# A decoder layer on one core: accumulating transfers from a negated cast, rotations moved into the products that need them, two copies on another engine

## The chip, the cores and the metric

The kernel runs on one core of a Trainium2 chip. A core has a matrix engine (PE, with its weight loads PEld), a vector engine (DVE), a scalar engine (ACT), a general engine (POOL) and an engine that here only issues transfers (SP). Each works through its own list of instructions in order and waits on semaphores for the others. Data moves between the chip's memory (HBM) and the core's on-chip memory (SBUF) by 16 DMA engines, whose transfers are issued from the queues of SP, ACT or POOL. Products of PE land in eight banks of PSUM, which DVE and ACT read.

The metric is the device time of one execution in microseconds; a measurement is the median of several.

## The reference

One layer for 256 positions and a width of 2048, all in float32:

```python
h = layer_norm(alpha * h + 0.5 * swiglu(h, w_ffn1_gu[i], w_ffn1_down[i]), ln_g[i, 0], ln_b[i, 0])
rq, rk, rv, rg, aq, ak, av, gate_r, gate_a = jnp.split(h @ w_in[i], SPLIT_POINTS, axis=-1)
rq = rotary(rq.reshape(B, S, RET_HEADS, RET_DK), positions, RET_DK, RET_THETA)
rk = rotary(rk.reshape(B, S, RET_HEADS, RET_DK), positions, RET_DK, RET_THETA) * (RET_DK ** -0.5)
...
ro = head_group_norm(retention_chunkwise(rq, rk, rv), ret_gn_g[i]).astype(h.dtype)
ret_branch = (jax.nn.silu(rg) * ro) @ w_ret_out[i]
...
att_branch = sliding_window_attention_sinks(aq, ak, av, att_sinks[i]) @ w_att_out[i]
mixed = (jax.nn.sigmoid(gate_r) * ret_branch + jax.nn.sigmoid(gate_a) * att_branch) @ w_mix_out[i]
h = layer_norm(alpha * h + mixed, ln_g[i, 1], ln_b[i, 1])
h = layer_norm(alpha * h + 0.5 * swiglu(h, w_ffn2_gu[i], w_ffn2_down[i]), ln_g[i, 2], ln_b[i, 2])
ple = jax.nn.sigmoid(h @ w_ple_gate[i]) * (p[i] @ w_ple_proj[i])
h = layer_norm(alpha * h + ple, ln_g[i, 3], ln_b[i, 3])
```

The FFNs have an inner width of 5632. Retention has 8 heads (128 for queries and keys, 256 for values), the attention 16 query heads and 4 key heads of 64. The rotary embedding turns pairs of a vector's elements by an angle that grows with the position, so it needs a table of cosines and sines for the 256 positions.

## The kernel before

**Split operands.** A float32 product is made of three products of a faster format: every operand is split into a high part (a rounded copy, made by ACT) and a low part (what is left, made by DVE as a subtraction), in `split` at line 100. `Sum.add` (line 417) then runs three matrix products: low times high (L426), high times high (L427), and, last, high times the weight's low part (L428). For features computed with the roles exchanged (`features_chunk`, names rqk and aqk) a chunk runs eight products with the weight's high part (L377) and then the low ones (L385).

**Weights.** All weights stream from HBM in chunks of 128 partitions x 1024 elements, 512 KB. A plan lists them in the order of use. `fill` looks at it after each chunk that PE has finished (`done`): it loads the next chunks on SP's queue into one of 46 slots, and makes (splits) the chunks whose turn is near, so that some four chunks stand made ahead of PE. Names say what a tile is: rf_gu is the raw chunk of an FFN's gate and up weights, hf_gu its high part, lf_gu its low part; rw_in_f and so on for the mixers' input weights.

**Kinds of units.** In the FFNs' gate and up products, column blocks of 512 are worked off unit by unit. Some units are plain. Some ("S", class `Seven`) save one of eight products by adding weight halves first (tiles uf_gu and vf_gu, lines 222 to 225). In some pairs ("F") the second chunk, the "up" one, is `Folded`: its low part is not subtracted by DVE. ACT writes the high part (L165) and then its negative into the low part's tile (L166), and POOL issues a transfer that adds the raw chunk to it on its way (L167), so that raw minus high is left. There are 43 such chunks. Column blocks end with sums of the partial results on DVE (evw, eve, line 1026).

**The order around the products.** The engines' lists follow the program text, so the text is the schedule. `run_side` is called after every chunk of the long products: it runs the next job of `side` (retention and attention steps) and one step of the first generator in `lazy`. In `lazy` stand `rotary_table` (the angles; name "r" for retention, "a" for attention; ten steps of small DVE instructions, two sines on ACT and a load of the positions on ACT's queue) and `sums_ahead` (line 271), which makes the sums of the "D" units of the second FFN early and stores them to HBM: per item two loads, four adds, two high parts on ACT, two subtractions (L300, L302) and four stores, in steps that are two or three chunks apart.

**The stages of `mixers`** are: the first value block (rv); eight groups of query and key features (rqk, four chunks each, groups 0 to 3 the queries, 4 to 7 the keys); three more value blocks of eight chunks; the retention gate (rg) with the heads' scores (rs) and outputs (ro) between its chunks; attention features (av, aqk); the four blocks of retention's outer gate (gt) with eight steps of the attention between them; two gate blocks of the attention side (ga0, ga1); then the output products. The retention table "r" is made in the first FFN's down projection, from its first unit on. After each rqk group, `rotated` joins its two PSUM halves (ACT copies one, DVE adds, `joined`) and rotates at once: a shuffle, two multiplications and an addition on DVE (lines 1127 to 1131). An attention step runs the scores (as), a softmax on DVE and ACT (asc, aes), a transposition by DMA (wat to mat), a copy back on ACT (apt, L197) and the output product (ao). The gate blocks gt are copied out of PSUM by ACT (sig, L1460). Ahead of the third and the fourth of them DVE makes sums of activations for `Seven` units (`forms_of`, gaf0 and gaf1, from L511 on).

Of the kernel before, what the change touches and what calls it, by code (L numbers as in the profile page):

```python
# [8 lines left out]
F32 = mybir.dt.float32  # L9
# [4 lines left out]
ALU = mybir.AluOpType  # L14
# [44 lines left out]
def layer(ctx: ExitStack, tc: tile.TileContext, io):  # L59
    nc = tc.nc  # L60
    sync, act, dve, pool, pe = nc.sync, nc.scalar, nc.vector, nc.gpsimd, nc.tensor
# [14 lines left out]
    def slot(shape, dt, name):  # L76
        return slots.tile(shape, dt, tag="slot", name=name)

    def half(name):
        return slot([P, 2, 256], F32, name)  # L80
# [23 lines left out]
    class Chunk:  # L104
# [18 lines left out]
        def make(self):  # L123
            self.make_hi()
            split(self.hi, self.lo, self.raw)
# [24 lines left out]
    class Folded:  # L150
# [11 lines left out]
        def make(self):  # L162
            c = self.chunk
            c.make_hi()
            act.copy(c.hi, c.raw)  # L165
            act.mul(c.lo, c.hi.bitcast(F32), -1.0)  # L166
            pool.dma_start(c.lo, c.raw, accum_op=ALU.add)  # L167

    class Turn:

# [100 lines left out]
    def sums_ahead(items, wait, every):  # L271


        def pause():
            for _ in range(every):
                yield

        pairs = [[Chunk(k) for k in items[0]]]
        for _ in range(wait):
            yield  # L280
        for j, (key, _) in enumerate(items):
            a, b = pairs.pop()
            b11, b21, b12, b22 = a.of(a.raw, 0), a.of(a.raw, 1), b.of(b.raw, 0), b.of(b.raw, 1)
            u, v = (slot([P, 2, 512], F32, w + a.name) for w in "uv")
            t1, t3, t2, t4 = (x.rearrange("p (g n) -> p g n", g=2) for x in (u[:, 0], u[:, 1], v[:, 0], v[:, 1]))
            parts = [slot([P, 2, 512], F32R, w + a.name) for w in ("hu", "lu", "hv", "lv")]
            uh, ul, vh, vl = parts
            away = [dram.tile([P, 2, 512], F32, name=f"{w}{a.name}") for w in ("hud", "lud", "hvd", "lvd")]
            put_by_sums[key] = away
            dve.tensor_tensor(t1, b11, b12, ALU.add)  # L290
            dve.tensor_tensor(t3, b12, b22, ALU.add)
            yield from pause()
            act.copy(uh, u)
            dve.tensor_tensor(t2, b11, t3, ALU.add)
            dve.tensor_tensor(t4, t2, b21, ALU.add)
            yield from pause()
            act.copy(vh, v)
            if j + 1 < len(items):
                pairs.append([Chunk(k) for k in items[j + 1]])
            dve.tensor_tensor(ul, u, uh, ALU.subtract)  # L300
            yield from pause()
            dve.tensor_tensor(vl, v, vh, ALU.subtract)  # L302
            for e in range(2):
                sync.dma_start(away[e], parts[e].bitcast(F32))
            yield from pause()
            for e in range(2, 4):
                sync.dma_start(away[e], parts[e].bitcast(F32))
# [48 lines left out]
        room["quiet"] = on  # L356

    side = []
    lazy = []
    idle = lambda: None  # L360

    def run_side(n=1):
        for _ in range(n):
            if side:
                side.pop(0)()
        if lazy and next(lazy[0], "end") == "end":
            lazy.pop(0)

    def features_chunk(key, n_k, rhs, ps):
        c, chunks = key[-1], n_k // 4  # L370
# [480 lines left out]
    trig = {}  # L851
# [16 lines left out]
    def rotary_table(nm):  # L868

        inv, sgn = (0, 2) if nm == "r" else (1, 3)  # L870
        pos_i = slot([P, S], I32, "pos_i" + nm)
        act.dma_start(pos_i, io["positions"].broadcast_to([P, S]))
        pos = slot([P, S], F32, "pos" + nm)
        yield
        dve.tensor_copy(pos, pos_i)
        table = slot([P, 2, S], F32, "trig" + nm)
        cos, sin = trig[nm] = table[:, 0, :], table[:, 1, :]
        w = slot([P, 4, S], F32, "rot" + nm)
        ang, n, na, nb = (w[:, j, :] for j in range(4))
        dve.tensor_scalar(ang, pos, cst[:, inv : inv + 1], None, ALU.mult)  # L880
        dve.tensor_scalar(n, ang, INV_2PI, MAGIC, ALU.mult, ALU.add)
        dve.tensor_scalar(n, n, MAGIC, None, ALU.subtract)
        dve.tensor_scalar(na, n, 1.0 / 2048.0, MAGIC, ALU.mult, ALU.add)
        dve.tensor_scalar(na, na, MAGIC, 2048.0, ALU.subtract, ALU.mult)
        dve.tensor_tensor(nb, n, na, ALU.subtract)
        yield
        for who, j in ((na, 0), (nb, 0), (na, 1), (nb, 1), (na, 2), (nb, 2), (na, 3)):
            dve.scalar_tensor_tensor(ang, who, -TWO_PI[j], ang, ALU.mult, ALU.add)
            if who is nb:
                yield  # L890
        yield
        dve.tensor_scalar(n, ang, 3.1415925, -3.1415925, ALU.min, ALU.max)
        yield
        act.activation(nb, n, AF.Sin)
        yield
        dve.tensor_scalar(sin, nb, cst[:, sgn : sgn + 1], None, ALU.mult)
        dve.tensor_scalar(na, ang, 1.5707963267948966, None, ALU.add)
        dve.tensor_scalar(n, na, 3.141592653589793, -6.283185307179586, ALU.is_gt, ALU.mult)
        dve.tensor_tensor(na, na, n, ALU.add)
        dve.tensor_scalar(na, na, 3.1415925, -3.1415925, ALU.min, ALU.max)  # L900
        yield
        act.activation(cos, na, AF.Sin)
        yield
# [47 lines left out]
    def ffn(name, i, ht, norm, keep, residual, keepers, away):  # L951
# [105 lines left out]
            return f  # L1057

        def before_unit(u):
            if u == 0 and name == "f1":  # L1060
                lazy.append(rotary_table("r"))
            g = u // 2 + 2
            others(2 * KF // 4 - max(0, KF // 4 - 1 - g) + (2 if u >= 10 else 0))
            if u % 2 == 0:
                if 2 <= u < 2 + 2 * len(SEVEN_DOWN):
                    at = u // 2 - 1
                    made[SEVEN_DOWN[at]] = seven_forms(raws[SEVEN_DOWN[at]], space[:, 2 * at], space[:, 2 * at + 1])
                if g < KF // 4:
                    convert(g)
            if u in (11, 12):  # L1070
                y[u - 11] = load_columns(residual, u - 11, name + "y")
# [44 lines left out]
    def joined(ps, name, dst=None):  # L1116
        lo = half(name + "lo")
        v = half(name + "v") if dst is None else dst
        for f in range(2):
            act.copy(lo[:, f], ps[f][:, S:])  # L1120
            dve.tensor_tensor(v[:, f], ps[f][:, :S], lo[:, f], ALU.add)
        return v

    def rotate(ps, name, dst, cos, sin, shuffle):
        q = joined(ps, name)
        qs = half(name + "sh")
        dve.stream_shuffle(qs, q, shuffle)
        c, s = (v[:, None, :].broadcast_to([P, 2, S]) for v in (cos, sin))
        dve.tensor_tensor(q, q, c, ALU.mult)
        dve.tensor_tensor(qs, qs, s, ALU.mult)  # L1130
        dve.tensor_tensor(dst, q, qs, ALU.add)

    SH_R = [(i + 16) % 32 for i in range(32)]
    SH_A = [i + 8 if i < 8 else i - 8 if i < 16 else i for i in range(32)]
# [35 lines left out]
        side.insert(n, job)  # L1170

    def mixers(ht, norm, residual, keepers, away):
        cos_r, sin_r = trig["r"]
        rhs = lambda k: (ht[:, k, :S], ht[:, k, S:])
        both_halves = lambda k: ht[:, k, :]
        rq = [slot([P, 4, S], F32, f"rq{j}") for j in range(2)]
# [1 line left out]

        def rotated(grp, ps):
            who = (rq, rk)[grp // 4][grp % 4 // 2]  # L1180
            rotate(ps, f"rr{grp}", who[:, grp % 2 * 2 : grp % 2 * 2 + 2, :], cos_r, sin_r, SH_R)

        rv = []

# [6 lines left out]
        ps = banks("rv0")  # L1191
# [5 lines left out]
        for c in range(FRONT, KD // 2):  # L1197
            u = take(("w_rv", 0, c))
# [2 lines left out]
        values(0, ps)  # L1201
        slots_for_weights(14)
        ahead = [(gu_keys("f2", j)(0, p), gu_keys("f2", j)(1, p)) for j in AHEAD for p in AHEAD[j]]
        lazy.append(sums_ahead(ahead[:2], 3, 2))
        lazy.append(rotary_table("a"))
        lazy.append(sums_ahead(ahead[2:5], 2, 2))
        lazy.append(sums_ahead(ahead[5:8], 2, 3))
        for grp in range(8):
            ps = banks(f"rqk{grp}")
            features_out([(("w_in_f", grp), ps)], KD, both_halves)  # L1210
            rotated(grp, ps)
        grp = 8
# [3 lines left out]
        for blk in range(1, 4):  # L1216
            ps = banks(f"rv{blk}")
# [97 lines left out]
        for h in range(0, HR, 2):  # L1315
            ps = banks(f"rg{h}")
# [6 lines left out]
            c = h // 2  # L1323
# [5 lines left out]
        ps = banks("av")  # L1329
# [119 lines left out]
        sig = []  # L1449
        for j in range(4):  # L1450
            def before(c, j=j):
                if c == 0 and j >= 2:
                    g = j - 2
                    made[g] = forms_of([ht[:, 4 * g : 4 * g + 4, :]], f"gaf{g}")

            ps = banks(f"gt{j}")
            paired_out(("w_in_f2", 21 + 2 * j), KD, rhs, ps, before)
            sig.append(slot([P, 2, 512], F32, f"sig{j}"))
            for t in range(2):
                act.copy(sig[-1][:, t], ps[t])  # L1460
        assert not side

        def mixer_block(name, units, keys, lhs):
# [38 lines left out]
        for b in range(2):  # L1502
# [3 lines left out]
            for n in range(2):  # L1506
                j = 2 * b + n
# [31 lines left out]
        ps = banks("mo2")  # L1539
# [4 lines left out]
        ps = banks("mo3")  # L1544
# [4 lines left out]
        for c in range(first):  # L1549
            u = take(("w_mix", 3, c))  # L1550
# [311 lines left out]
```

## Time and profile before

| | |
|---|---|
| median of three runs | 2252.4 us (2251.03 to 2253.74) |
| the profiled execution | 2251.64 us |
| its span | 2249.9 us, so 1.7 us lie outside the span |
| granted PE clock | 0.999 |
| HBM read, written | 484.43 MB, 29.36 MB |
| mean transfer rate | 248 GB/s |

The page divides the span into 40 slices. In its row for PE every slice but the last shows nine tenths or more; DVE's digits lie between seven and nine in most slices, ACT's between four and seven. A matrix product on 512 columns shows as 0.39 us, but such products overlap in the pipeline and start 0.22 to 0.23 us apart. In rows of stretches, the number behind an engine's busy time in brackets is its count of instructions. In rows of waits stand the waiting instruction, what ended the wait, and then the total, the number and the longest. In the chain of waits each piece is followed back to what released it; "issue" is time in which nothing that the profile shows was waited for.

### The profile page before, as it was taken

What the parts mean: (1) busy time and instruction counts of PE and PEld (TensorE: products, weight loads), DVE (VectorE), ACT (ScalarE), POOL (GpSimd) and SP (SyncE); (2) the same over time, 40 slices, a digit from 0 to 9 for tenths busy, and PEclk for the clock granted to TensorE, in tenths of its full rate; (3) what the DMA queues carried; (4) which work ended last, traced back from release to release, by engine and by line L of the source; (5) the groups of instructions that cost most, each with busy time, mean ns of one, the idle gap of its engine ahead of it and who ended that gap; (6) DMA issues with size and microseconds to landing.
All of it is one profiled execution on the core that took longest, in us unless ns stands there. A gap on an engine that the chain in (4) does not pass through costs nothing.

```text
span 2249.9 us, 28922 instructions
## 1 busy us (share of the span) xinstructions
PE 2230.0 (99%) x10191; PEld 1845.7 (82%) x10191; DVE 1976.5 (88%) x2575; ACT 1406.5 (63%) x1640; POOL 39.7 (2%) x52
## 2 busy tenths in 40 slices
PE   9999999999999999999999999999999999999998
PEld 8888878888888888888778888888888778888887
DVE  6999999999989887888789778789999899889877
ACT  6777777766555444656776466456667677655533
POOL 0000000000000000000000000000000000000000
PEclk9999999999999999999999999999999999999999
DMA  9989998965677878767666578788989898555771
GB/s 321 244 270 254 246 257 239 256 220 186 220 284 260 292 282 306 223 239 231 187 189 234 178 229 296 301 283 274 315 271 294 275 250 262 188 215 210 286 266 72
DMA packets 292267, 557.14 MB, mean 248 GB/s; under 512 B 92045, under 2 KB 96525, under 8 KB 292121
## 3 DMA queue, kind: packets, MB, share of 16 engines
q1 hardware_dynamic: 283944, 530.16, 70.5%
q0 software_dynamic: 6192, 22.55, 5.3%
q10 hardware_dynamic: 1984, 2.58, 0.4%
q8 instruction: 80, 1.31, 0.2%
q14 instruction: 67, 0.54, 0.1%
HBM read 484.43 MB, written 29.36 MB: 228 GB/s over the span
## 4 chain that ended last, share of the span: by engine, by line
PE 75%; DVE 10%; DMA 6%; ACT 4%; issue 4%; SPq 0%; ACTq 0%; DVEq 0%; POOLq 0%
DMA lf_gu<-rf_gu 3%; PE rqk L377 3%; PE f1g L428 2%; PE f1g L427 2%; PE f1g L426 2%; PE f2g L427 2%; PE f2g L426 2%; PE f2g L428 2%; PE f1u L428 2%; PE f1u L427 2%; PE f2u L428 2%; PE f1u L426 2%; DVE lw_in_f L102 2%; PE f2u L427 2%; PE f2u L426 2%
## 5 line engine op out<-in xcount | busy, mean ns | idle before, releaser
L102 DVE TENSOR_TENSOR lf_gu<-rf_gu,hf_gu 128x1024 fp32r<-128x1024 f32 (+1 forms) x225 | 267.7, 1210 | 20.5 <-ACT hf_gu L101 19.7
L101 ACT CAST hf_gu<-rf_gu 128x1024 fp32r<-128x1024 f32 (+1 forms) x225 | 228.5, 1039 | 33.3 <-DMA rf_gu<-in_f_gu 32.9
L102 DVE TENSOR_TENSOR lf_down<-rf_down,hf_down 128x1024 fp32r<-128x1024 f32 x150 | 178.8, 1220 | 19.1 <-ACT hf_down L101 18.2
L102 DVE TENSOR_TENSOR lw_in_f<-rw_in_f,hw_in_f 128x1024 fp32r<-128x1024 f32 x140 | 167.4, 1219 | 28.2 <-ACT hw_in_f L101 27.7
L101 ACT CAST hf_down<-rf_down 128x1024 fp32r<-128x1024 f32 x150 | 151.9, 1049 | 49.3 <-DMA rf_down<-in_f_down 19.5
L101 ACT CAST huf_gu<-uf_gu 128x1024 fp32r<-128x1024 f32 x76 | 80.1, 1054 | 120.6 <-DVE uf_gu L223 111.9
L101 ACT CAST hw_in_f<-rw_in_f 128x1024 fp32r<-128x1024 f32 x140 | 140.2, 1049 | 5.2 <-PE rg L428 1.5
L101 ACT CAST hvf_gu<-vf_gu 128x1024 fp32r<-128x1024 f32 x76 | 80.1, 1054 | 32.1 <-DVE vf_gu L225 31.3
L102 DVE TENSOR_TENSOR luf_gu<-uf_gu,huf_gu 128x1024 fp32r<-128x1024 f32 x76 | 92.6, 1218 | 0.0
L102 DVE TENSOR_TENSOR lvf_gu<-vf_gu,hvf_gu 128x1024 fp32r<-128x1024 f32 x76 | 92.5, 1218 | 0.0
L426 PE MATMUL f1g<-hf_gu,xt 128*128 128x512 f32 x232 | 90.7, 391 | 0.0
L428 PE MATMUL f1g<-lf_gu,xt 128*128 128x512 f32 x232 | 90.5, 390 | 0.1
L427 PE MATMUL f1g<-hf_gu,xt 128*128 128x512 f32 x232 | 90.5, 390 | 0.0
L426 PE MATMUL f2g<-hf_gu,ht 128*128 128x512 f32 x214 | 83.5, 390 | 0.0
L428 PE MATMUL f2g<-lf_gu,ht 128*128 128x512 f32 x214 | 83.3, 389 | 0.0
L427 PE MATMUL f2g<-hf_gu,ht 128*128 128x512 f32 x214 | 83.3, 389 | 0.0
L428 PE MATMUL f1u<-lf_gu,xt 128*128 128x512 f32 x192 | 75.4, 393 | 4.1 <-DMA lf_gu<-rf_gu 4.1
L427 PE MATMUL f1u<-hf_gu,xt 128*128 128x512 f32 x192 | 74.7, 389 | 0.0
L426 PE MATMUL f1u<-hf_gu,xt 128*128 128x512 f32 x192 | 74.7, 389 | 0.0
L167 POOL DMA_DIRECT2D lf_gu<-rf_gu x43 | 37.3, 868 | 1852.8 <-DMA rf_gu<-in_f_gu 1240.9
L428 PE MATMUL f2u<-lf_gu,ht 128*128 128x512 f32 x168 | 66.0, 393 | 2.7 <-DMA lf_gu<-rf_gu 2.5
L426 PE MATMUL f2u<-hf_gu,ht 128*128 128x512 f32 x168 | 65.8, 392 | 0.0
(1471 smaller groups left out, 6788.9 us busy)
## 6 DMA issues: line engine op xcount, KB each, us to landing
rf_gu<-in_f_gu SPq DMA_DIRECT2D x360, 512.0 KB
rf_down<-in_f_down SPq DMA_DIRECT2D x176, 512.0 KB
rw_in_f<-in_w_in_f SPq DMA_DIRECT2D x148, 512.0 KB
lf_gu<-rf_gu POOLq DMA_DIRECT2D x43, 512.0 KB, 7.5
rw_rv<-in_w_rv SPq DMA_DIRECT2D x32, 512.0 KB
rw_ret<-in_w_ret SPq DMA_DIRECT2D x32, 512.0 KB
rw_mix<-in_w_mix SPq DMA_DIRECT2D x32, 512.0 KB
rw_pg<-in_w_pg SPq DMA_DIRECT2D x32, 512.0 KB
```

Of the source, the lines that this page charges most:

```text
L101: act.copy(dst_hi, src)
L102: (lo_engine or dve).tensor_tensor(dst_lo, src, dst_hi, ALU.subtract)
L167: pool.dma_start(c.lo, c.raw, accum_op=ALU.add)
L377: pe.matmul(ps[f], hi[:, kk, f * P : (f + 1) * P], rhs(k), start=k == 0, stop=k == n_k - 1,)
L426: pe.matmul(o, al, bh, start=first, stop=False)
L427: pe.matmul(o, ah, bh, start=False, stop=False)
L428: pe.matmul(o, ah, bl, start=False, stop=self.left == 0)
```

## The change

There are four edits:

- `Folded.make`: ACT first writes the negated raw chunk, rounded, into the low part's tile, POOL's adding transfer is issued, and then ACT writes the high part. Rounding is the same for both signs, so the values are the same.
- The retention table is no longer made in the first FFN's down projection. In `mixers` a second list, `slow`, runs beside `lazy`, one step of each at each chunk. It holds the retention table, the rotations, then the attention's table. `rotated` only joins, into the tile that is kept; `rotations` turns it in place later, in the order 0, 4, 1, 5, 2, 6, 3, 7, as soon as both table and group are there, two chunks apart at least.
- `lazy` holds eight items of `sums_ahead` as three and five, all with steps two chunks apart, where it held two, the attention's table, three, and three with steps three chunks apart. The last two items stay where they were.
- Of the four gate blocks gt, DVE copies the third and fourth out of PSUM.

```diff
         def make(self):
             c = self.chunk
             c.make_hi()
+            act.mul(c.lo, c.raw, -1.0)
+            pool.dma_start(c.lo, c.raw, accum_op=ALU.add)
             act.copy(c.hi, c.raw)
-            act.mul(c.lo, c.hi.bitcast(F32), -1.0)
-            pool.dma_start(c.lo, c.raw, accum_op=ALU.add)
...
     side = []
-    lazy = []
+    lazy, slow = [], []
...
-        if lazy and next(lazy[0], "end") == "end":
-            lazy.pop(0)
+        for jobs in (slow, lazy):
+            if jobs and next(jobs[0], "end") == "end":
+                jobs.pop(0)
...
         def before_unit(u):
-            if u == 0 and name == "f1":
-                lazy.append(rotary_table("r"))
...
-    def rotate(ps, name, dst, cos, sin, shuffle):
-        q = joined(ps, name)
+    def turn_by_angle(q, name, dst, cos, sin, shuffle):
         qs = half(name + "sh")
         dve.stream_shuffle(qs, q, shuffle)
         c, s = (v[:, None, :].broadcast_to([P, 2, S]) for v in (cos, sin))
         dve.tensor_tensor(q, q, c, ALU.mult)
         dve.tensor_tensor(qs, qs, s, ALU.mult)
         dve.tensor_tensor(dst, q, qs, ALU.add)
+
+    def rotate(ps, name, dst, cos, sin, shuffle):
+        turn_by_angle(joined(ps, name), name, dst, cos, sin, shuffle)
...
         def rotated(grp, ps):
             who = (rq, rk)[grp // 4][grp % 4 // 2]
-            rotate(ps, f"rr{grp}", who[:, grp % 2 * 2 : grp % 2 * 2 + 2, :], cos_r, sin_r, SH_R)
+            to = who[:, grp % 2 * 2 : grp % 2 * 2 + 2, :]
+            joined(ps, f"rr{grp}", to)
+            unturned[grp] = to
+
+        unturned = {}
+
+        def rotations():
+            for grp in (0, 4, 1, 5, 2, 6, 3, 7):
+                while grp not in unturned:
+                    yield
+                to = unturned.pop(grp)
+                turn_by_angle(to, f"rr{grp}", to, *trig["r"], SH_R)
+                yield
+                yield
...
-        lazy.append(sums_ahead(ahead[:2], 3, 2))
-        lazy.append(rotary_table("a"))
-        lazy.append(sums_ahead(ahead[2:5], 2, 2))
-        lazy.append(sums_ahead(ahead[5:8], 2, 3))
+        def angles():
+            yield from rotary_table("r")
+            yield from rotations()
+            yield from rotary_table("a")
+
+        slow.append(angles())
+        lazy.append(sums_ahead(ahead[:3], 3, 2))
+        lazy.append(sums_ahead(ahead[3:8], 2, 2))
...
-                act.copy(sig[-1][:, t], ps[t])
+                (act.copy if j < 2 else dve.tensor_copy)(sig[-1][:, t], ps[t])
```

More of the change, by code (lines that the diff above doesn't have):

```diff
@@ L1172, in mixers @@
     def mixers(ht, norm, residual, keepers, away):
-        cos_r, sin_r = trig["r"]
         rhs = lambda k: (ht[:, k, :S], ht[:, k, S:])
```

## The prediction

> **What bounds the kernel now.** I read the page first, then the waits of the matrix engine (PE), then the chain of waits, then each engine in order of time where the change acts.
>
> ```profile
> span 2249.9 us, 28922 instructions
> PE 2230.0 (99%) x10191; PEld 1845.7 (82%) x10191; DVE 1976.5 (88%) x2575; ACT 1406.5 (63%) x1640; POOL 39.7 (2%) x52
> ```
>
> PE is busy for 2230.0 of 2249.9 us, and the change alters no product. So it can win only some of the 19.9 us in which PE stands still, and it loses wherever it makes a new stall. The waits of PE (total, times, longest) say who ends its stalls:
>
> ```profile
> PE f1u L428 <- DMA lf_gu<-rf_gu: 4.1, 6, 1.8
> PE ao L1423 <- ACT apt L197: 3.2, 2, 2.5
> PE f2u L428 <- DMA lf_gu<-rf_gu: 2.5, 3, 1.8
> ...
> PE ro L1253 <- DVE rsp L102: 0.5, 1, 0.5
> ```
>
> The largest part, 6.6 us in nine stalls, is PE at the third product of an "up" chunk, whose low part an accumulating transfer delivers. Next are 3.2 us before the attention output.
>
> **1. The accumulating transfer starts earlier.** The chain ahead of the longest stall (start, length, what):
>
> ```profile
> 309.82 0.96 ACT hf_gu L165
> 310.78 0.02 issue
> 310.80 1.07 ACT lf_gu L166
> 311.87 0.35 issue
> 312.22 9.53 DMA lf_gu<-rf_gu
> 321.75 0.04 issue
> 321.79 0.50 PE f1u L428
> ```
>
> ACT writes the high part, then its negative, and then POOL issues; PE takes the chunk when the transfer has landed. After the change the negated cast is first and reads the raw chunk, so it no longer stands behind the high part. It ends one ACT instruction earlier, 1.07 us (310.80 to 311.87), and issue and landing move with it. Nothing is added: the same two ACT instructions, the same transfer, and no step moves past another on SP's or POOL's queue. The high part comes about 1.07 us later, at 311.87. Its first reader is two products ahead of the stalled one: 321.79 less the 1.8 us stall and 0.6 us for the two products, 319.4. So 7.5 us cover the delay; without them it would be a stall of 1.07 us in each of 43 chunks. ACT's later work starts when it did before.
>
> The two longest stalls shrink by 1.07 us each. The other seven sum to (4.1 - 1.8) + (2.5 - 1.8) = 3.0 us, and the largest of them is this one, below 1.07, so all seven go:
>
> ```profile
> 403.65 0.39 PE L426 MATMUL f1u<-hf_gu,xt 128*128 128x512 f32 x1
> 403.87 0.39 PE L427 MATMUL f1u<-hf_gu,xt 128*128 128x512 f32 x1
> 405.13 0.50 PE L428 MATMUL f1u<-lf_gu,xt 128*128 128x512 f32 x1 [0.87 <-DMA lf_gu<-rf_gu]
> 405.47 0.39 PE L426 MATMUL f1u<-hf_gu,xt 128*128 128x512 f32 x1
> ```
>
> A stall costs more than its idle time. Starts are 0.22 us apart when PE streams; here the steps are 1.26 and 0.34, so 1.16 us are lost for 0.87 us of idleness, some 0.27 us to drain and restart. Sum: 2 x 1.07 + 3.0 + 7 x 0.27 = **-7.0 us**. Ends: 0 if the landing doesn't move, and -(6.6 + 9 x 0.27) = -9.0 if all nine stalls go. I take -7.0, since PE starts 0.04 us after the landing.
>
> ```profile
> DVE evw L1026 <- PE f1u L428: 6.1, 7, 1.4
> 300.00:350.00 50.00, 48.19 (x213) 39.58 (x212) 45.77 (x55) 36.80 (x40) 2.61 (x3) 1.00 0.86 237
> DMA to landing us min/median/max: 4.9/7.5/10.3
> ```
>
> DVE makes the other low parts; the first row has it waiting for PE at the end of seven column blocks. So PE is its clock, and the gain isn't eaten there. The second row is 50 us with such stalls (busy PE, PEld, DVE, ACT, POOL; clock, DMA share, GB/s): the DMA engines are 0.86 busy, and in the third the time from issue to landing spreads over 5.4 us.
>
> A rule of the Trainium skill speaks against me here: DMA: Bandwidth & Descriptors, section Queues, rings and completion order, says that each DMA engine takes turns between its queues, a packet at a time. By it a landing follows the loads queued beside it as much as its own issue, and this term could be anything from 0 to -7.0. The spread in the last row agrees with such sharing, but shows no limit.
>
> **2. Retention's angles and rotations move.** The table of angles for retention leaves the first down projection, where PE waits for nothing, and so gains nothing there. It costs DVE 6.76 us, the first row:
>
> ```profile
> 466.00:498.00 32.00, 6.76 (x19) 0.83 (x2) 1.00 0.66 226
> 748.83 0.75 DVE L1127 STREAM_SHUFFLE rr1sh<-rr1v 128x512 f32<-128x512 f32 x1
> ...
> 751.55 2.35 DVE L102 TENSOR_TENSOR lw_in_f<-rw_in_f,hw_in_f 128x1024 fp32r<-128x1024 f32 x2
> L290 DVE TENSOR_TENSOR uf_gu<-rf_gu,rf_gu 128x512 f32<-128x512 f32 x2 | 1.4, 684 | 0.0
> ```
>
> The table now fills the first ten chunks of the query and key products, its position load on ACT's queue ahead of the casts there; the attention's table (as long) goes from there into the value products. A rotation is 2.72 us (748.83 to 751.55). It was at the end of each group and now comes at chunks 11, 21, 23, 25, 27, 29, 31 and 33, since the fixed order takes group 4 second. Its first reader follows 24 chunks of value products later. The weight sums made ahead for the second FFN run beside this list instead of taking turns with it: an item is four adds of 0.68 us and two subtractions of 1.18 (half of 2.35), 5.1 us, and by 925 us eight are made instead of six, each with two loads and four stores on SP's queue. So DVE gets 6.8 + 10.2 = 17.0 us more between 727 and 925 us:
>
> ```profile
> 727.00:816.00 89.00, 89.00 (x512) 78.35 (x511) 77.65 (x118) 39.39 (x54) 0.00 (x0) 1.00 0.79 281
> 727.00:925.00 198.00, 198.00 (x1004) 169.06 (x1003) 160.58 (x235) 97.57 (x120) 0.00 (x0) 1.00 0.82 283
> 740.37 2.35 DVE L102 TENSOR_TENSOR lw_in_f<-rw_in_f,hw_in_f 128x1024 fp32r<-128x1024 f32 x2
> ...
> 747.35 2.29 PE rqk L377 x10
> ```
>
> DVE is busy for 160.6 of these 198 us, so 37.4 us are free and 17.0 fit. The tight place is chunks 21 to 32. The 89 us hold eight groups of four chunks, 11.1 us each; in that time DVE has four low parts (4.7), a join (0.8, 748.03 to 748.83 in the row before the shuffle), two rotations (5.4) and some 2 us of sums, 12.9 us. Over three groups it falls behind by 3 x 1.8 = 5.4 us. The cover is the lead: a group's first low part is done by 741.5, the group's products begin at 747.35, and eight high products (1.8 us) come ahead of the first low one: 7.6 us. So **0 us**, with 2 us to spare; beyond them each further us would be a us of stall. The value products let DVE catch up. The position cast now waits on DVE for its load, with low parts behind it, and ACT's two sines wait for DVE with high-part casts behind them: the same lead covers both, and ACT is free for 49.6 of the first 89 us. The transfers are 0.82 busy there, against 0.86 in the stretch of the first FFN shown, so the sums' loads and stores have room.
>
> After 925 us the reverse holds: the two items that DVE made then are gone, and with them the 0.5 us wait of the output product (ro): **-0.6 us** with part of a restart; ends 0 and -0.8.
>
> **3. DVE copies two gate blocks.** ACT's copy was free where the third block ends, and DVE's is not:
>
> ```profile
> 1132.07 1.08 ACT L1460 COPY sig<-gt 128x512 f32<-128x512 f32 x2
> 1134.60 1.05 ACT L101 CAST gaf1h<-sums 128x1024 fp32r<-128x1024 f32 x1 [1.45 <-DVE sums L502]
> 1131.83 1.15 DVE gaf1w L511
> ...
> 1154.52 0.66 PE ao L1423 x4
> L1332 DVE COPY akv<-av x2: 392/404/415, 995.2 to 995.5; 128x256 f32<-128x256 f32 x2
> ```
>
> ACT idles 1.45 us right after its copy, waiting for DVE's sums. The third and fourth rows are the ends of a chain from gaf1w through the softmax to the output product, all DVE, ACT and one transfer, and PE stands 2.5 us at its end. The two DVE copies go in ahead of gaf1w. The nearest copy out of PSUM takes 0.40 us for 256 columns; for 512 I take 0.66 each, **+1.3 us** on that chain (ends 0.8 and 1.6: the pair as if of 256 columns, and twice that). The last block's copies fall here:
>
> ```profile
> 1158.00:1229.00 71.00, 71.00 (x315) 58.80 (x314) 70.00 (x84) 42.52 (x48) 0.00 (x0) 1.00 0.60 195
> 1226.60 1.22 DVE L102 TENSOR_TENSOR lvw_in_f<-vw_in_f,hvw_in_f 128x1024 fp32r<-128x1024 f32 x1
> 1228.69 0.39 PE L428 MATMUL ga1s<-lvw_in_f,gaf1h 128*128 128x512 f32 x1
> ```
>
> DVE works 70 of 71 us, and the last low part comes 0.87 us before its use. 1.3 us in front of it leave a stall of 0.4, with restart **+0.7 us** (ends 0 and 1.6).
>
> **The sum:** -7.0 + 0 - 0.6 + 1.3 + 0.7 = -5.6 us. The profiled execution took 2251.6 us (1.7 outside its span), so 2246.0; the median of the three runs, 2252.4, is 0.8 above it, so **2246.8 us**.
>
> **Rivals.** (a) The earlier issue doesn't land earlier, being held by the traffic. For: the spread of 5.4 us is five times the gain. Against: every row's stall ends at a landing, and nothing but the cast holds the issue. The page of the Trainium skill named under part 1 (DMA: Bandwidth & Descriptors) stands for it. Then +2.0 - 0.6 = +1.4, 2253.8 us. (b) Slower: DVE becomes the bound in the query and key products. Its free 37.4 us may lie behind waits for PE and ACT at group ends, where added work can't use them; the 2.0 us to spare speak for it, the free share against. It decides as soon as a low part is over 7.6 us late. If none of the gaps can be used, 17.0 - 7.6 = 9.4 us of stalls, less the 5.6 won: +3.8, 2256.2 us. (c) The copies cost nothing, as DVE, rid of the late sums, is ahead by the attention, and the 2.5 us stall goes with its restart: -7.6 - 2.8 = -10.4, 2242.0 us. Against it: gaf1w's chain starts long after the last sum.
>
> **How the numbers follow.** Forecast 0.58, (a) 0.22, (b) 0.12, (c) 0.08. The forecast's own range is 2243.4 (-9.0 - 0.8 + 0.8 + 0) to 2248.6 (-7.0 + 1.6 + 1.6). The whole range reaches to (a) and (c), 2241.5 to 2254.0, and leaves (b) out. A measurement tells 0.2%, 4.5 us, from no change, so faster means below 2247.9: most of the forecast (0.50) and (c), 0.58. The same is most of (a) and the forecast's weak end, 0.27; slower is (b) and a little of (a), 0.15.
>
> **What would show it.** Right: PE's waits for the transfers fall from 6.6 to about 1.5 us, with the negated cast ahead of the high part's; the wait for apt grows from 3.2 to about 4.5; no wait of PE in the query, key and value products. Wrong: the transfer waits stay, with times to landing 1 us longer (a); PE waits for DVE there (b); the wait for apt is gone (c).

## The result and the profile after

| | before | changed |
|---|---|---|
| median | 2254.99 us of 11 runs (2251.03 to 2258.21) | 2248.14 us of 11 runs (2246.49 to 2249.51) |
| profiled execution | 2251.64 us | 2248.75 us |

The ratio is 0.9971, 95% interval 0.9962 to 0.9979: 6.5 us faster (4.7 to 8.6). The two profiled executions differ by 2.9 us only. A second profile of each kernel, further down, shows why.

The page of the changed kernel, then its waits of PE (total, times, longest). In `Folded.make` L165 is now the negated cast, L166 POOL's issue and L167 the high part. The code from `run_side` on moved by one line (L428 is now L429), that of `mixers` by 17 (L1423 is L1440):

```profile
span 2247.0 us, 29022 instructions
PE 2230.2 (99%) x10191; PEld 1847.2 (82%) x10191; DVE 1978.1 (88%) x2579; ACT 1399.7 (62%) x1636; POOL 39.6 (2%) x52
```

```profile
PE ao L1440 <- ACT apt L197: 2.7, 2, 2.4
PE f2u L429 <- DMA lf_gu<-rf_gu: 1.8, 2, 1.5
...
PE f27s L429 <- DVE lf_gu L102: 1.0, 1, 1.0
PE f1u L429 <- DMA lf_gu<-rf_gu: 0.9, 1, 0.9
PE gt L429 <- DVE lw_in_f L102: 0.8, 1, 0.8
```

PE works as long as before (2230.2 us with a clock dip in it, which the first profile of before lacks; see the last section). Its waits for accumulating transfers fell from 6.6 us in nine stalls to 2.7 in three. The wait of ro is gone, no wait stands in the query, key and value products. Two waits are new: f27s for a low part (1.0) and gt for a low part (0.8).

The three rows of the transfers and of stretches that answer to those of before (in the stretches: busy PE, PEld, DVE, ACT, POOL; clock, DMA share, GB/s):

```profile
DMA to landing us min/median/max: 4.9/7.8/10.3
```

```profile
300.00:350.00 50.00, 50.00 (x222) 41.40 (x221) 47.70 (x58) 38.20 (x42) 2.60 (x3) 1.00 0.91 250
727.00:816.00 89.00, 89.00 (x505) 78.03 (x504) 81.34 (x122) 42.04 (x56) 0.00 (x0) 1.00 0.84 302
727.00:925.00 198.00, 198.00 (x1003) 168.93 (x1002) 175.72 (x269) 101.60 (x126) 0.00 (x0) 1.00 0.90 314
```

The time from issue to landing grew by 0.3 us in the median, so part of the earlier start is lost on the way. In 300 to 350 us PE has no wait left. DVE has 15.1 us more between 727 and 925 (175.72 less 160.58) and PE still never waits there.

The attention's end, from the timelines of DVE and PE of the changed kernel:

```profile
1126.12 1.28 DVE L1477 COPY sig<-gt 128x512 f32<-128x512 f32 x2
1127.31 1.22 DVE L512 TENSOR_TENSOR gaf1w<-ht 128x1024 f32<-128x1024 f32 x1
```

```profile
1138.20 0.50 PE L429 MATMUL gt<-lw_in_f,ht 128*128 128x512 f32 x1 [0.78 <-DVE lw_in_f L102]
...
1149.99 1.13 PE L1440 MATMUL ao<-apt,akv 128*64 128x256 f32 x4 [2.38 <-ACT apt L197]
```

The pair of copies takes 1.28 us and holds gaf1w up by 1.19 (1127.31 less 1126.12). The delay shows first as a stall of a gate product whose low part is queued behind it on DVE; the wait for apt, with PE itself now later, stays as long as it was.

### The profile page after: what moved, and what is told of

It is laid out like the page before. It is cut to its first block, busy times and chain, and to the rows that moved or that the text cites. A ratio compares the mean times of both kernels' runs of the same rounds, so it can differ in the third digit from the quotient of the medians.

```text
span 2247.0 us, 29022 instructions
## 1 busy us (share of the span) xinstructions
PE 2230.2 (99%) x10191; PEld 1847.2 (82%) x10191; DVE 1978.1 (88%) x2579; ACT 1399.7 (62%) x1636; POOL 39.6 (2%) x52
## 4 chain that ended last, share of the span: by engine, by line
PE 93%; DMA 2%; issue 2%; DVE 1%; ACT 1%; POOL 0%; ACTq 0%; POOLq 0%; DVEq 0%
PE rqk L378 3%; PE f1g L429 3%; PE f1g L427 3%; PE f1g L428 3%; PE f2g L428 2%; PE f2g L427 2%; PE f2g L429 2%; PE f1u L429 2%; PE f1u L427 2%; PE f1u L428 2%; PE f2u L429 2%; PE f2u L428 2%; PE f2u L427 2%; PE aqk L378 2%; PE f2d L429 2%
## 5 line engine op out<-in xcount | busy, mean ns | idle before, releaser
L428 PE MATMUL f1g<-hf_gu,xt 128*128 128x512 f32 x232 | 90.5, 390 | 0.0
L429 PE MATMUL f1g<-lf_gu,xt 128*128 128x512 f32 x232 | 90.4, 390 | 0.0
L429 PE MATMUL f2g<-lf_gu,ht 128*128 128x512 f32 x214 | 83.3, 389 | 0.0
L428 PE MATMUL f2g<-hf_gu,ht 128*128 128x512 f32 x214 | 83.3, 389 | 0.0
L429 PE MATMUL f1u<-lf_gu,xt 128*128 128x512 f32 x192 | 74.9, 390 | 0.9 <-DMA lf_gu<-rf_gu 0.9
L428 PE MATMUL f1u<-hf_gu,xt 128*128 128x512 f32 x192 | 74.7, 389 | 0.0
L166 POOL DMA_DIRECT2D lf_gu<-rf_gu x43 | 37.3, 867 | 1849.7 <-DMA rf_gu<-in_f_gu 1215.8
L429 PE MATMUL f2u<-lf_gu,ht 128*128 128x512 f32 x168 | 65.6, 391 | 1.8 <-DMA lf_gu<-rf_gu 1.8
```

What stands on the lines that cost most here:

```text
L428: pe.matmul(o, ah, bh, start=False, stop=False)
L429: pe.matmul(o, ah, bl, start=False, stop=self.left == 0)
```

## The experiments

Differences in us are the ratio's times the median of before, with its 95% interval.

### One edit at a time

**Only the order inside `Folded.make`:**

```diff
+            act.mul(c.lo, c.raw, -1.0)
+            pool.dma_start(c.lo, c.raw, accum_op=ALU.add)
             act.copy(c.hi, c.raw)
-            act.mul(c.lo, c.hi.bitcast(F32), -1.0)
-            pool.dma_start(c.lo, c.raw, accum_op=ALU.add)
```

> Only the order inside Folded.make is changed: negated cast, transfer, then high part. My theory: this edit alone carries the gain, 5 to 9 us below the kernel before (-7.0 by the prediction's sum), and PE's waits for lf_gu fall from 6.6 us in nine stalls to about 2 to 3 us in two or three. Rival (the landing follows the traffic, not the issue): within 1.5 us of before, the waits stay near 6 us, and the time from issue to landing grows by 1 us from its median of 7.5 us.

Measured: -4.7 us (-6.8 to -2.9). Its waits of PE:

```profile
PE f27s L428 <- DVE lf_gu L102: 1.8, 1, 1.8
PE f1u L428 <- DMA lf_gu<-rf_gu: 1.5, 2, 0.9
...
PE f2u L428 <- DMA lf_gu<-rf_gu: 1.3, 1, 1.3
```

The transfers' waits are 2.8 us in three stalls, so this edit does what the changed kernel shows; rival (a) is out. But f27s stalls for 1.8 us. Where that comes from is seen in DVE's timeline of before and then of the changed kernel:

```profile
1774.69 0.69 DVE L222 TENSOR_TENSOR uf_gu<-rf_gu,rf_gu 128x512 f32<-128x512 f32 x1 [6.64 <-DMA rf_gu<-in_f_gu]
```

```profile
1772.96 0.69 DVE L222 TENSOR_TENSOR uf_gu<-rf_gu,rf_gu 128x512 f32<-128x512 f32 x1 [5.94 <-DMA rf_gu<-in_f_gu]
```

In both DVE waits 6 us for a weight load from HBM, which comes 1.7 us earlier in the changed kernel, while PE's first f27s product, in the rows of PE's timeline in the same order, is there 2.6 us earlier:

```profile
1758.90 0.39 PE L426 MATMUL f27s<-hf_gu,ht 128*128 128x512 f32 x1
```

```profile
1756.29 0.39 PE L427 MATMUL f27s<-hf_gu,ht 128*128 128x512 f32 x1
```

The load doesn't follow PE all the way, and the difference, 0.9 us, is the new wait. In the run of this edit alone PE is there 4.2 us and the load 2.5 us earlier than in before, and the wait is 1.8. So part of what is won ahead of this place is given back at it. What holds the load is not shown.

**Only table, rotations and the two lists** (`slow` and `lazy` as in the diff of the change; `Folded.make` and the copies as before):

> Only the moved table, the moved rotations and the denser list of sums are changed. My theory: between -1.5 and 0 us against before (the 0.5 us wait of ro for rsp goes, no wait of PE for DVE appears in the query, key and value products). Rival (the added DVE work is paid by PE): +2 us or more, with waits of rqk for lw_in_f. Second rival: the two tables taken out of the first down projection and out of the first mixer products are what gained, -3 us or more, through something the waits of PE do not show.

Measured: -1.1 us (-3.2 to +0.7). The wait of ro is gone and no wait stands in rqk or rv; DVE's busy time in 727 to 925 us is 173.52. f27s waits 0.7 us for lf_gu here too, although the transfers are issued as before; so the earlier transfers are not the only cause of that wait. The first rival falls. The second's -3 lies at the edge of the interval, and nothing in the profile speaks for it.

**Only the copies:**

```diff
-                act.copy(sig[-1][:, t], ps[t])
+                (act.copy if j < 2 else dve.tensor_copy)(sig[-1][:, t], ps[t])
```

> Only the copies of the third and fourth gate block go to DVE. My theory: +0.5 to +1.5 us against before; a wait of gt for lw_in_f of about 0.8 us appears, gaf1w starts about 1.2 us later, and the wait of ao for apt plus that of gt is 0.6 us longer than the 3.2 us of before. Rival (ACT, freed of the copies, is what the changed kernel gains by): -0.5 us or below, with the wait for apt shorter.

Measured: +3.4 us (+1.1 to +5.6), with these waits, and the last low part of ga1 in the timelines of DVE and PE:

```profile
PE ao L1423 <- ACT apt L197: 3.3, 2, 2.6
...
PE gt L428 <- DVE lw_in_f L102: 0.8, 1, 0.8
```

```profile
1229.15 1.22 DVE L102 TENSOR_TENSOR lvw_in_f<-vw_in_f,hvw_in_f 128x1024 fp32r<-128x1024 f32 x1
```

```profile
1230.42 0.50 PE L428 MATMUL ga1s<-lvw_in_f,gaf1h 128*128 128x512 f32 x1
```

The copies cost time, and ACT gains nothing by them. The new stall of gt with its restart is 1.1 us (0.8 and 0.27), apt 0.1 more; in ga1 PE starts 0.05 us after the low part is done, where 0.87 us were left before: it just touches. These come to 1.2 us, and so do the spans of the two profiles (2251.1 less 2249.9 us), neither of which has a clock dip. That the measured value is larger is not explained by this profile: its execution, 2252.91 us, is the second fastest of twelve, whose median is 2256.12.

### The changed kernel with ACT copies, and second profiles of both kernels

```diff
-                (act.copy if j < 2 else dve.tensor_copy)(sig[-1][:, t], ps[t])
+                act.copy(sig[-1][:, t], ps[t])
```

> The changed kernel with all four gate blocks copied by ACT again. My theory: 0.5 to 1.5 us below the changed kernel, so 7 to 8.5 us below before, without the wait of gt for lw_in_f and with a wait for apt like that of before. Rival (the DVE copies cost nothing or help): equal to the changed kernel or above it.

> The changed kernel itself, to stand beside the others on one chip. Theory: 5 to 8 us below before, with the waits of its first profile (gt for lw_in_f 0.8, ao for apt 2.4, lf_gu below 3 us together). Whether the granted clock falls behind the 2.4 us stall differs from one execution to the next: it did in the first profile (0.83 in 1150 to 1160 us).

> The kernel before itself, for a second profile. Its first profile took 2251.64 us, 2 to 3 below its medians (2253.6 to 2255.0), and shows no clock dip behind its three stalls of 1.8 us or more. My theory: a typical execution of it has one or two dips of 1.7 us behind those stalls (13 of 22 such stalls in ten other profiles have one), so a profile that takes some 2253 to 2256 us shows them, with waits for lf_gu near the 6.6 us of the first. Rival (the spread is in the transfers): no dip, and the waits for lf_gu are 9 us or more in a profile of that time. A profile near 2251 us with neither tells nothing.

Measured: with ACT copies -6.8 us (-9.5 to -4.1), without the wait of gt; the changed kernel again -7.2 (-9.9 to -4.7); before against itself +0.9 (-1.1 to +2.9). So the copies' price of about 1 us in the changed kernel, argued from the wait, is not seen in times. The profiles say more. The stretch behind the wait for apt, in before's second profile (2254.26 us, its median), the changed kernel's second (2248.06), and the one with ACT copies (2245.91):

```profile
1150.00:1160.00 10.00, 7.52 (x30) 5.55 (x31) 7.85 (x11) 9.47 (x15) 0.00 (x0) 0.83 0.87 250
```

```profile
1150.00:1160.00 10.00, 10.00 (x43) 7.88 (x40) 9.27 (x13) 6.41 (x9) 0.00 (x0) 0.83 0.36 121
```

```profile
1150.00:1160.00 10.00, 10.00 (x45) 8.28 (x45) 9.79 (x15) 6.73 (x9) 0.00 (x0) 1.00 0.39 119
```

The column before the DMA share is the granted clock: 0.83, 0.83 and 1.00. A dip of this size costs some 1.6 us (an estimate, worked out in the last section). It followed the 2.4 us stall in the changed kernel's first profile and not in before's first. Like must be compared with like: with the dip in both, spans are 2252.5 and 2246.3, 6.2 us apart; without it in both (before's first, and ACT copies), 2249.9 and 2244.1, 5.8 apart. The transfers' waits in before's second profile:

```profile
PE f1u L428 <- DMA lf_gu<-rf_gu: 5.2, 6, 1.8
...
PE f2u L428 <- DMA lf_gu<-rf_gu: 2.1, 2, 1.8
```

They sum to 7.3 us and to 2.5 in the changed kernel's second. So the theory holds for one of the three stalls: one dip, none behind the two of 1.8 us. What decides is shown in the last section.

### Transfers issued later

The kernel before with one, then two more ACT casts ahead of the issue (both results are overwritten):

```diff
             act.copy(c.hi, c.raw)
+            act.mul(c.lo, c.raw, -1.0)
             act.mul(c.lo, c.hi.bitcast(F32), -1.0)
```

> The kernel before, with one more ACT cast of 1.07 us between the high part and the negated cast of each folded chunk, so that every accumulating transfer is issued 1.07 us later (the extra cast's result is overwritten). My theory (the landing follows the issue): the opposite of the change and larger, since more chunks cross from spare time into a stall. From before's trace: nine stalls grow by 1.07 (9.6 us), twelve landings that had less than 1.07 us to spare become stalls of 6.6 us together, with 0.27 each for restarting 3.2 us: +19 us if the whole delay arrives at the landing, +13 if only the 0.7 of it that the median from issue to landing suggests (7.45 us before, 7.8 with the earlier issue). Rival (the traffic sets the landing): within 3 us of before.

> The kernel before with two more ACT casts (2.14 us) between the high part and the negated cast of each folded chunk (their results are overwritten); the run with one more cost 14 us, 9.4 of it in waits for lf_gu and some 8 in five clock dips of 1.7 us. My theory (landing follows issue, and each stall of 1.8 us or more loses another 1.7 us in about 13 of 22 cases): waits for lf_gu grow by another 20 us or more, since nearly every chunk has less than 3 us to spare, to 30 to 45 us together, with 6 to 12 dips; 30 to 55 us above before. Rival (the traffic sets the landings and the first run's cost was mostly the clock): waits below 25 us, below 25 us above before.

Measured: +13.1 us (+9.9 to +16.0) and +30.2 (+27.0 to +33.6). Waits and times to landing, first with one more cast, then with two:

```profile
PE f1u L429 <- DMA lf_gu<-rf_gu: 8.4, 6, 3.4
PE f2u L429 <- DMA lf_gu<-rf_gu: 7.6, 4, 2.8
```

```profile
DMA to landing us min/median/max: 4.6/6.4/9.6
```

```profile
PE f1u L430 <- DMA lf_gu<-rf_gu: 18.6, 11, 3.6
PE f2u L430 <- DMA lf_gu<-rf_gu: 6.4, 4, 3.0
```

```profile
DMA to landing us min/median/max: 4.5/6.5/11.1
```

The sign and the steps are those of the theory, the sizes lie below it: the waits grew to 16.0 and 25.0 us, where 18 to 23 (6.6 plus 16.2, or 0.7 of it) and 30 or more were expected. A transfer issued later takes less time: the median from issue to landing falls from 7.5 to 6.4. Over all 43, the mean from the first cast of a chunk to the landing is 9.9 and 9.7 us in the two profiles of before, 8.9 in both of the changed kernel (issue 1.09 earlier, landing 0.8 to 1.0), 10.1 with one cast more and 11.2 with two. So landings follow the issue only in part: of the 1.09 us of the earlier issue 0.8 to 1.0 arrive, of the 1.0 us of one cast more 0.2 to 0.4, and of the 2.1 us of two 1.3 to 1.5. The mean hides that the late ones got later: the longest stall grew from 1.8 to 3.4 us. The added casts delay ACT's other work as well, but PE waited for a high part only once, 1.1 us, with two casts more. Most of the rest of the cost is the clock: five stalls of 2.0 to 3.4 us in the first of these profiles are each followed by a dip, and six of 2.3 to 3.7 us in the second (in each, one of them is the wait for apt). For the first, 9.4 us of waits and five dips of 1.6 come to 17.4, where its span is 16.7 us longer than that of before's first profile (2266.6 less 2249.9), which has no dip.

### Taking gaf1 off the last attention output

With ACT copies, gaf1's sums are moved: to the third quarter of the fourth block, to the last of the third, to the second of the second, and there with gaf0's in the first block. The first of the four:

```diff
-                if c == 0 and j >= 2:
+                if (j, c) in ((2, 0), (3, 2)):
                     g = j - 2
```

> The changed kernel with all gate blocks copied by ACT and with gaf1's sums moved from the start of the fourth gate block to its third quarter, behind the softmax of the last attention step. My theory (DVE's sums delay that softmax, not the copies alone): the 2.3 us wait of ao for apt goes or falls below 0.5, 2.5 us below the same kernel without the move, 9 to 10 below before; and if long stalls trip the PE clock in part of the executions (10 us at a granted 0.83, some 1.7 us, as seen behind three of the stalls of 1.8 to 2.4 us), 1 us more in the median. Rival (the wait moves: gaf1's high part now stands ahead of apt on ACT): no gain.

> As the run with the moved sums, but gaf1's sums go earlier, to the last quarter of the third gate block. My theory: the last attention step's softmax starts some 3.7 us earlier as well, but the step before it is delayed by about as much and has 1.9 us to spare before its ao, so a new wait of up to 2 us appears there: between 0 and 2.5 us below the changed kernel with ACT copies. Rival: no new wait, the same gain as with the sums moved back.

> The changed kernel with all gate blocks copied by ACT and with gaf1's sums moved to the second quarter of the second gate block, into the attention step that has 8.1 us to spare before its ao. My theory (DVE's and ACT's work for gaf1 is what delays the last attention output, wherever it stands in the last two blocks): the 2.3 us wait of ao for apt falls below 0.5 and no other wait of ao grows; 2.5 us below the changed kernel with ACT copies, 9 to 10 us below before, and the clock dip that follows a stall of 1.8 us or more cannot come there. Rival (something else in that chain comes last, such as the transposition): the wait stays above 1.5 us and there is no gain.

> As the run before it, and gaf0's sums move as well, from the start of the third gate block to the second quarter of the first, into an attention step with 9.9 us to spare. My theory: the 0.3 us wait of ao for apt in the fifth step goes too, 0 to 0.5 us below the run with gaf1 alone moved. Rival: the sums now meet attention steps and low parts that DVE has no room for, and a wait of gt or ao for DVE appears; 0.5 us or more above that run.

Measured, in this order: -6.1 (-8.6 to -3.8), -6.8 (-9.5 to -4.1), -4.7 (-6.8 to -2.7), -2.0 us (-4.3 to 0.0). None is clearly better than the changed kernel. My theory failed each time: the wait for apt came back in another step or behind another instruction. Its row in the four profiles:

```profile
PE ao L1440 <- ACT apt L197: 3.7, 2, 3.4
```

```profile
PE ao L1440 <- ACT apt L197: 3.1, 2, 2.8
```

```profile
PE ao L1440 <- ACT apt L197: 4.2, 1, 4.2
```

```profile
PE ao L1440 <- ACT apt L197: 4.5, 1, 4.5
```

ACT's timeline tells why for two of them. First the sums late, in the fourth block; then gaf1's sums in the second block:

```profile
1142.59 1.05 ACT L101 CAST gaf1h<-sums 128x1024 fp32r<-128x1024 f32 x1 [2.61 <-DVE sums L503]
...
1147.28 1.95 ACT L197 COPY apt<-mat 128x768 uint16<-128x768 uint16 x2
```

```profile
1109.98 0.21 ACT L1393 ACTIVATE aes<-aes 128x4 f32<-128x4 f32 x1 [3.09 <-DVE aes L1386]
...
1112.78 1.95 ACT L197 COPY apt<-mat 128x768 uint16<-128x768 uint16 x2
```

In the first, apt stands on ACT behind gaf1's high part, which waits for DVE. In the second, apt of the fifth attention step stands behind the exponentials of the sixth, which wait 3.1 us for DVE. The spare time that I read at one step's ao was not free: ACT takes things in the order of the text, and the next step's work is ahead of this step's copy.

## Why the prediction was right, and where its steps were off

The time came out 1.3 us above the forecast (the difference to before as 6.5 us, where 5.6 were forecast), with the sign, the edit that carries it, and the absence of new waits in the query and key products as said. That the sum came so close is in part luck. By the second profiles the transfers brought 1.1 us less than forecast and the stall of f27s, which the forecast lacks, cost 1.1 with its restart; against that the copies cost 0.9 us less than forecast, the waits for apt are 0.5 shorter, and smaller waits went. The terms, with what stood in their place:

- **The transfers, -7.0.** The mechanism is shown, by the single edit and, in the other direction, by the later issues. The size: -4.7 by that edit's runs; by the two second profiles the idle time falls by 7.3 - 2.5 = 4.8 us and eight stalls become four, with 0.27 each -5.9. Of the step's reasoning, "issue and landing move with it" held for 0.8 to 1.0 us of 1.09. "All seven go" did not: a stall of 0.5 us at 238 us grew to 0.9 in the changed kernel's first profile, although its transfer was issued earlier; before's second profile has 1.1 us there, so it varies between executions. And "the gain isn't eaten there" did not: f27s stalls for 0.8 to 1.0 us in the changed kernel's two profiles, and 1.8 in that of the edit alone (0.7 of it appears with the moved angles alone). The restart of 0.27 us comes out of the prediction's rows as 0.29 (1.16 less 0.87), which changes the sum by 0.1. The rule of the Trainium skill that was set against this step (DMA: Bandwidth & Descriptors, section Queues, rings and completion order) is not borne out in its extreme: of the 1.09 us, all but 0.1 to 0.3 arrive. The later issues, of whose first 1.0 us only 0.2 to 0.4 arrive, lean more its way. Whether turn-taking at the DMA engines is what takes the rest is not shown.
- **Rotations, 0 with 2 us to spare, and ro, -0.6.** Right: the move alone gave -1.1 (-3.2 to +0.7), and ro's wait is gone. The reserve was mis-sized. The tightest place behind the first chunk is the last one; its low part and its first low product in the changed kernel, from the timelines of DVE and PE:

```profile
801.36 1.22 DVE L102 TENSOR_TENSOR lw_in_f<-rw_in_f,hw_in_f 128x1024 fp32r<-128x1024 f32 x1
```

```profile
808.77 0.99 PE L386 MATMUL rqk<-ht,lw_in_f 128*128 128x256 f32 x7
```

  6.2 us are left (808.77 less 802.58). DVE does fall behind where the two rotations per group stand, from a lead of 13.5 us for the low part used at 786.4 to this, 7.3 us. But it starts from 13.5, not from the 7.6 that I read at one group's start, because it had run ahead in the groups before, which the prediction left out.
- **The copies, +1.3 and +0.7.** The pair takes 1.28 us, as estimated (2 x 0.66), and delays gaf1w by 1.19. The place was wrong: not a longer wait for apt (forecast 4.5, found 2.7) but a stall of gt before it, as that product's low part was queued behind on DVE; I had followed only the chain to apt. In ga1, the spare time of 0.87 us shrank to 0.05 with the copies alone, and no stall showed in the changed kernel. There the clock dip of 1.6 us held PE back, and DVE was 1.38 us early. The profile of the copies alone gives +1.2 in place of +2.0, their runs +3.4 (1.1 to 5.6), and the two kernels that differ in the copies only, -6.8 and -7.2, show no price. So the size of this term stays open.

The three single edits sum to -2.4 us with an uncertainty of nearly 4, against -6.5 for the whole. Whether they help each other or the copies' +3.4 is too large was not settled. The stalls themselves account for most of it: from before's second profile to the changed kernel's, all of PE's waits over 0.15 us fall from 14.8 us in 18 to 10.3 in 14, which with 0.27 for each restart is 5.5 of the 6.2 us between their spans.

Rival (b) is out: DVE took 15.1 us more in the stretch and PE never waited. Rival (c) is out as well: the 2.4 us stall stayed although the late sums are gone. The four attempts to remove it point to the order of the work on ACT and DVE as what sets it.

## To carry to other kernels

An asynchronous transfer that ends stalls should be issued before any work that doesn't feed it; count what it wins by the landings, not by the issue, and look for the next load that doesn't follow PE. Spare time at one place of an in-order queue is only free if nothing behind it is awaited: list what is queued behind the new instruction, on the engine itself and on the engine that waits for its result. Two profiles of different executions may differ by more than the change; compare stall by stall, and the clock beside them: here the same stall had a dip behind it in one execution and none in the next.

## What the hardware showed

After a stall PE can run at half speed for a few microseconds. PE in the changed kernel's second profile, right after the 2.36 us wait:

```profile
1150.59 0.80 PE L427 MATMUL ga0a<-hw_in_f,ht 128*128 128x512 f32 x1
1151.19 0.63 PE L428 MATMUL ga0a<-hw_in_f,ht 128*128 128x512 f32 x1
1151.62 0.63 PE L429 MATMUL ga0a<-lw_in_f,ht 128*128 128x512 f32 x1
```

Starts are 0.43 us apart instead of 0.23. In the 14 profiles of this case, such a dip followed all 8 stalls of 2.7 us or more, 14 of the 24 between 1.8 and 2.7, and 1 of the 15 between 1.2 and 1.8 (that one with a second stall of 0.8 us right behind it). A dip lasts 3.41 us (three of the 23 last twice as long), so that after a stall below 3.4 us it costs, as an estimate, some 1.6 us more than the restart: 3.41 times (1 - 0.23/0.43).

The length of the stall doesn't decide alone; how it lies in time does. The traces keep the moments at which the granted clock changed. In every profile all of them are whole multiples of 3.413 us apart, on a grid that lies differently in each execution. Cut along that grid, the window of the wait for apt and the next one in before's second profile (busy PE first, the clock before the DMA share; in so short a stretch the share can pass 1, as a packet counts whole where it starts):

```profile
1152.87:1156.28 3.41, 0.93 (x10) 0.58 (x9) 1.88 (x3) 3.13 (x4) 0.00 (x0) 1.00 0.98 332
1156.28:1159.70 3.42, 3.42 (x8) 2.70 (x9) 3.34 (x5) 3.27 (x6) 0.00 (x0) 0.50 0.82 270
```

and the three windows around the same stall in before's first:

```profile
1149.98:1153.39 3.41, 2.03 (x9) 1.31 (x7) 3.41 (x4) 3.07 (x5) 0.00 (x0) 1.00 1.10 229
1153.39:1156.81 3.42, 2.29 (x14) 1.74 (x15) 1.80 (x4) 3.32 (x7) 0.00 (x0) 1.00 1.02 337
1156.81:1160.22 3.41, 3.41 (x16) 2.82 (x15) 3.30 (x7) 2.99 (x4) 0.00 (x0) 1.00 0.44 162
```

In before's second profile, PE stood still for 2.48 us of one window, and the next ran at half speed. In its first, the stall of 2.52 us was split into 1.39 and 1.13, and nothing followed. So it is in all 14 profiles, some 9,170 windows: behind each of the 24 windows with 1.81 us or more of idle PE, the clock was halved for the next. Behind windows with 1.64 us or less it never was, but for one (1.06 us) that ran at half speed itself. Between them, 1.69 us had a dip, and 1.70 and 1.75 had none.

The Trainium skill (TensorE: Matmul & The Clock Gate, section Part 1: The HAM clock gate) says that the array's clock is halved after an idle window of about 3.4 us, and full again after a busy one, and that the window runs freely. The half speed, the length of the window and its running free agree with these traces; but a window need not be idle throughout: 1.81 us of its 3.41 sufficed here, about half.
